# Strassen's seven products for the up-projections of a gated MLP, in written order, with tiles moved

## The chip, the cores and the metric

The kernel runs on one core of a Trainium2 chip. The time is device microseconds of one execution; 2133.42 is the median of three runs of the kernel before (2128.67 to 2134.68). TensorE (PE in the profile) multiplies matrices into PSUM; VectorE (DVE), ScalarE (ACT) and GpSimd (POOL) do the elementwise work, and GpSimd reads no PSUM here. SyncE (SP) issues nearly all transfers. Each engine works through its own queue of instructions in order and waits on semaphores of the others.

## The reference

One layer of an encoder over 1024 positions of width 1024, in float32. The change touches its last part, a gated MLP of hidden width 2816 with a convolution over three positions in the gate:

```python
h = rms_norm(x, norm_ffn_g[l])
gp = dwconv_centered(h @ w_ffn_gate[l], ffn_conv_w[l], ffn_conv_b[l])
x = x + (jax.nn.silu(gp) * (h @ w_ffn_up[l])) @ w_ffn_down[l]
```

Before it come an input projection, latent attention over eight heads, a bidirectional RWKV-7 recurrence, and a gated merge of the two, `x = x + (gates[:, :, 0] * y_a + gates[:, :, 1] * y_b) @ w_merge[l]`.

## The kernel before

Data lie transposed: 128 channels on the partitions, 1024 positions along them. A float32 operand of a product is split into a rounded high part and the rest (`split`, L162: a cast on ScalarE at L163, a subtraction on GpSimd or VectorE at L164), and a product is three matmuls, high times high, high times low and low times high (`mmk`, L245, matmuls at L248, L249 and L251), each 128 x 128 weights against 512 columns. A block of 128 rows and all 1024 positions is therefore six matmuls.

The work runs in four stages. Phase A projects the input and prepares the operands of both branches. Phase B runs the recurrence over chunks, with attention and other dense products in between, in an order that a small planner works out (`LATENCY`, `DENSE`, `PACE`, and the loop over `units`); only PE's order is fixed by hand (`manual_schedule` for PE), the other engines' order is made by the scheduler. The gates of the mixture are written to DRAM by `gate_done` (the stores of the last two tiles of 128 channels go out on GpSimd's queue, the others on SP's). Phase C computes the second branch's part of the mixture (`branch`, eight tiles of four blocks) and the merge: for each of eight tiles of 128 channels, eight blocks with the operands `yh`, `yl`; then VectorE adds the residual (L1485), ScalarE scales it to `h2h` (L1488), VectorE takes the rest `h2l` (L1489), and squares are summed on ScalarE and GpSimd (L1493, L1494).

Phase D is the MLP. `GROUPS` cuts the 22 tiles of 128 hidden channels into four groups. For each tile f, PE forms the gate's product `pg` and the up-projection's `pu`, eight blocks each with the operands `h2h`, `h2l`, in PSUM tiles of 1024 columns (`big4`, four of them in all eight banks). VectorE multiplies `pg` by 1/rms (L1517), ScalarE and VectorE do the convolution (L1522 to L1524), ScalarE the silu, GpSimd multiplies by 1/rms (L1527), VectorE by `pu` (L1528), and the result is split into `sh`, `sl`. After a group the down projection adds its products to the residual `x2`: for each of eight output tiles, as many blocks as the group has tiles, and one addition on VectorE (L1535). In the last group each output tile is stored as it is done (L1537). The sum of squares over channels is a float32 product with ones (`mm32`, L192) after the first gate product. Weights come as 128 x 512 floats, 256 KB, two loads ahead (`wload`, L168, its transfer at L171).

The allocation stacks tiles from the left and from the right of each partition's memory, in steps of 32 bytes. On the left `cst`, `b64r` and `vec` take 391 + 128 + 192 floats, so that what follows (`x2`, `yh`, `yl`, `sh`, `sl`) starts 32 bytes past a multiple of 128; on the right the weights and the places `hh0` to `hl7` of `h2h`, `h2l` start 96 past one.

Of the kernel before, what the change touches and what calls it, by code (L numbers as in the profile page):

```python
# [19 lines left out]
D = 1024  # L20
# [4 lines left out]
C = 64  # L25
# [4 lines left out]
GROUPS = ((0, 6), (6, 12), (12, 17), (17, 22))  # L30
# [18 lines left out]
# How long a step of phase B takes to be ready after it has left TensorE's queue, in ns  # L49
# [39 lines left out]
def block_kernel(ctx: ExitStack, tc: tile.TileContext, a):  # L89
# [15 lines left out]
    # ScalarE functions, grouped by table set in the order of emission  # L105
# [4 lines left out]
    def act(out, in_, func, **kw):  # L110
# [3 lines left out]
        if name != cur["set"]:  # L114
            ld = S.preload_act_table_set(name)
            for g in cur["group"]:
                tc.add_manual_dep(ld.ins, g.ins.name, NOSYNC, reason="table set order")
# [3 lines left out]
        i = S.activation(out, in_, func, **kw)  # L121
        tc.add_manual_dep(i.ins, cur["load"].ins.name, NOSYNC, reason="table set order")
# [7 lines left out]
    nc.sync.dma_start(vec, a["vecs"])  # L130
    ident = cst[:, C_ID:C_ID + 128]
# [121 lines left out]
    # x enters the products as x * g; the evacuation of a product multiplies by 1 / rms(x).  # L253
# [119 lines left out]
    # Products with the projection's tiles: a step per 128 rows.  # L373
# [18 lines left out]
    def parted(x, hi=None, lo=None):  # L392
        """512 columns as the sum of two that a pass each carries."""
# [16 lines left out]
    # The rest of the phase runs as threads between the steps of the projection. A thread yields  # L410
    # what its next part waits for: a key of DELAY, or a tile that has to be there.
# [33 lines left out]
    def key_rope():  # L445
# [25 lines left out]
        # the rows that pad the heads' operands to 128: zeros, and the ones that meet the row of maxima  # L471
# [184 lines left out]
    def parts(idle=False):  # L656
        """The parts that are due of the threads that run; a lane runs so many of its threads at a time."""
# [46 lines left out]
    # ---------------------------------------------------------------- phase B  # L704
# [926 lines left out]
```

## Time and profile before

| | |
|---|---|
| median of three runs | 2133.42 us |
| the profiled execution: its span, first to last instruction | 2126.6 us |
| PE busy | 1958.1 us (92%) |
| phase A, 0 to about 320 us: PE busy | 283.8 us |
| phase B, 320 to 1230 us: PE busy | 786.4 us |
| phase D, 1394.2 us to the end | 732.4 us |
| mean granted PE clock | 0.962 |

The page's second part cuts the span into 40 slices of 53 us and gives the busy share of each engine in tenths. A group of the fifth part names line, engine, operation, output and inputs with shapes, the count, busy time, the mean of one in ns, then idle time before it and what ended that. Matmuls overlap, so their durations (389 ns) are longer than the step from one start to the next; the step is read from the starts in the timeline. Weight loads (PEld) are records of their own and run beside the matmuls.

### The profile page before, as it was taken

Reading aid. Unit: us, or ns where it says so; the run is one execution under the profiler, and the core shown is the slowest. Engines: PE = TensorE matmul, PEld = TensorE weight load, DVE = VectorE, ACT = ScalarE, POOL = GpSimd, SP = SyncE. Lnnn points to the kernel's source line nnn. Section 1 sums busy time; section 2 is a strip of 40 time slices with the busy share of each in tenths; the row PEclk is TensorE's granted clock in tenths of the full one; section 3 lists DMA queues with packets and bytes.
Section 4 is the critical chain, followed back from the end, with each engine's and each line's share of the span. In section 5 each row is a group of like instructions: output and inputs, shape, how many; then the busy total and the mean of one; then the engine's idle time right before and its main releaser. Section 6 shows DMA issues by size and latency. Waiting matters only on the chain.

```text
span 2126.6 us, 31745 instructions
## 1 busy us (share of the span) xinstructions
PE 1958.1 (92%) x12280; PEld 1507.2 (71%) x12280; DVE 997.4 (47%) x1560; ACT 843.1 (40%) x1459; POOL 871.8 (41%) x763
## 2 busy tenths in 40 slices
PE   7799999899898779888779999999999999999999
PEld 5566667677666556556557678888888888888887
DVE  8566766626474768667773235232212321221321
ACT  4676564123233546565547644232212211221221
POOL 7344546133233646564546432433323322332331
PEclk9899999899998989999989999999999999999999
DMA  3047447354344334352433685111111111111113
GB/s 144 34 140 230 145 162 219 104 145 113 98 130 125 78 108 106 104 135 79 100 86 91 205 303 189 50 45 50 43 53 50 50 43 52 50 39 56 50 38 117
DMA packets 212551, 221.09 MB, mean 104 GB/s; under 512 B 114152, under 2 KB 138792, under 8 KB 212400
## 3 DMA queue, kind: packets, MB, share of 16 engines
q1 hardware_dynamic: 212080, 218.01, 33.4%
q8 instruction: 97, 1.59, 0.3%
q0 software_dynamic: 320, 1.05, 0.1%
q14 instruction: 54, 0.44, 0.1%
HBM read 151.20 MB, written 63.60 MB: 101 GB/s over the span
## 4 chain that ended last, share of the span: by engine, by line
PE 51%; DVE 7%; DMA 3%; issue 1%; SPq 1%; POOL 0%; ACT 0%; DVEq 0%; POOLq 0%; ACTq 0%
PE b L251 13%; PE b L248 13%; PE b L249 13%; DMA IN<-dn 2%; DVE Ti L815 2%; DVE tm L811 2%; DVE mx L1151 1%; PE po L1179 1%; PE st L1205 1%; PE po L1181 1%; PE st L1207 1%; PE po L1180 1%; PE st L1206 1%; PE ct L972 1%; PE st L248 1%
## 5 line engine op out<-in xcount | busy, mean ns | idle before, releaser
L164 POOL TENSOR_TENSOR wlo<-wraw,whi 128x512 fp32r<-128x512 f32 x248 | 306.8, 1240 | 792.6 <-ACT whi L163 788.7
L163 ACT CAST whi<-wraw 128x512 fp32r<-128x512 f32 x248 | 145.2, 586 | 652.4 <-PE b L249 462.1
L248 PE MATMUL b<-h2h,whi 128*128 128x512 f32 x704 | 274.3, 390 | 0.0
L249 PE MATMUL b<-h2l,whi 128*128 128x512 f32 x704 | 273.9, 389 | 0.0
L1217 POOL TENSOR_TENSOR pl<-pe,ph 128x512 fp32r<-128x512 f32 x128 | 169.6, 1327 | 131.2 <-ACT ph L1216 128.6
L251 PE MATMUL b<-h2h,wlo 128*128 128x512 f32 x704 | 216.7, 389 | 0.0
L248 PE MATMUL st<-hh,whi 128*128 128x512 f32 x408 | 176.0, 431 | 15.2 <-ACT hh L275 9.0
L249 PE MATMUL st<-hl,whi 128*128 128x512 f32 x408 | 164.7, 404 | 0.5 <-DVE hl L276 0.5
L248 PEld LDWEIGHTS b<-h2h,whi 128*128 128x128 f32 x704 | 132.2, 188 | 27.7 <-issue 0.2
L249 PEld LDWEIGHTS b<-h2l,whi 128*128 128x128 f32 x704 | 132.2, 188 | 27.7 <-issue 0.2
L251 PEld LDWEIGHTS b<-h2h,wlo 128*128 128x128 f32 x704 | 132.2, 188 | 27.5
L251 PE MATMUL st<-hh,wlo 128*128 128x512 f32 x408 | 140.9, 400 | 0.5 <-POOL wlo L164 0.5
L248 PE MATMUL b<-sh,whi 128*128 128x512 f32 x352 | 138.8, 394 | 0.0
L249 PE MATMUL b<-sl,whi 128*128 128x512 f32 x352 | 138.7, 394 | 0.0
L1535 DVE TENSOR_TENSOR x<-b,x 128x1024 f32<-128x1024 f32 x32 | 39.2, 1225 | 197.6 <-PE b L251 197.6
L811 DVE TENSOR_TENSOR tm<-IN,Ti 128x126 f32<-128x126 f32 (+22 forms) x248 | 91.2, 368 | 77.5 <-DMA IN<-dn 71.3
L251 PE MATMUL b<-sh,wlo 128*128 128x512 f32 x352 | 110.4, 394 | 0.0
L248 PEld LDWEIGHTS st<-hh,whi 128*128 128x128 f32 x408 | 79.6, 195 | 43.0 <-issue 9.8
L815 DVE TENSOR_TENSOR Ti<-Ti,tm 128x126 f32<-128x126 f32 (+22 forms) x248 | 104.3, 421 | 6.6
L1517 DVE TENSOR_TENSOR u<-b,rs 128x1024 f32<-128x1024 f32 x22 | 26.9, 1224 | 169.6 <-PE b L251 158.4
L1216 ACT CAST ph<-pe 128x512 fp32r<-128x512 f32 x128 | 79.1, 620 | 64.5 <-PE po L1181 61.3
L980 POOL TENSOR_TENSOR sm<-RR,pcs 64x128 f32<-64x128 f32 x112 | 47.6, 425 | 126.4 <-DVE RR L1002 105.2
(333 smaller groups left out, 4159.1 us busy)
## 6 DMA issues: line engine op xcount, KB each, us to landing
wraw<-w_in SPq DMA_DIRECT2D x64, 256.0 KB
wraw<-w_fg SPq DMA_DIRECT2D x44, 256.0 KB
wraw<-w_fu SPq DMA_DIRECT2D x44, 256.0 KB
ld<-d_x SPq DMA_DIRECT2D x32, 256.0 KB
wraw<-w_fd SPq DMA_DIRECT2D x32, 256.0 KB
d_gate<-gt SPq DMA_DIRECT2D x28, 256.0 KB
xt<-xT SPq DMA_DIRECT2D x8, 512.0 KB
d_s<-sg SPq DMA_DIRECT2D x8, 512.0 KB
```

The costliest lines, as they stand in the source:

```text
L163: S.copy(hi, x)
L164: (eng or G).tensor_tensor(out=lo, in0=x, in1=hi.bitcast(F32), op=sub)
L248: nc.tensor.matmul(o, wh, xh[:, hs], start=first, stop=False)
L249: nc.tensor.matmul(o, wh, xl[:, hs], start=False, stop=False)
L251: nc.tensor.matmul(o, wl, xh[:, hs], start=False, stop=last)
L811: t = V.tensor_tensor(out=tm[:, 0:nt, 0:nj], in0=IN[:, s, s + 1:32][:, :, None].to_broadcast([128, nt, nj]), in1=Ti[:, s, 0:nj][:, None, : ...
L815: V.tensor_tensor(out=Ti[:, s + 1:32, 0:nj], in0=Ti[:, s + 1:32, 0:nj], in1=tm[:, 0:nt, 0:nj], op=add)
L980: state["pool"] = G.tensor_tensor(out=sm[hs], in0=RR[hs, :, h, 0, :], in1=pcv[hs, i // 4, :, i % 4, None].to_broadcast([64, 2, C]), op=mult)
L1216: S.copy(ph, pe)
L1217: G.tensor_tensor(out=pl, in0=pe, in1=ph.bitcast(F32), op=sub)
L1517: V.tensor_tensor(out=u, in0=pg, in1=rs2, op=mult)
L1535: V.tensor_tensor(out=x2[:, j, :], in0=ps, in1=x2[:, j, :], op=add)
```

## The change

Phase D's two up-projections of a tile are read as one product of a 2 x 2 matrix of blocks (up and gate weights, each in two halves of 512 input channels) with a 2 x 2 matrix of blocks of `h` (two halves of channels, two halves of 512 positions). Its eight block products are replaced by seven, in Winograd's form of Strassen's method: `B11`, `B21`, `B22` are blocks of `h`, `U1` to `U4` sums and differences of blocks, made once during the merge; the sums of the weights are made for every tile on GpSimd (`sums_next`, `diffs_next` and the subtraction of `s2`) and split on ScalarE and VectorE (`parts`). A `quarter` is one such product, four blocks of 128 rows against 512 positions, twelve matmuls into one PSUM bank. The results come as sums that build on each other in the banks `ba`, `bb`, `bc`: VectorE reads a partial sum, PE adds the next quarter onto it.

Every engine's order in this block is the written one (`manual_schedule` for all five), the table loads too. The first two tiles run together ahead of the loop, with the last merge tile's evacuation, and the rest of `U4`'s making, among them. From f = 2 each tile's loop also does half of the down products of the pair of tiles before, in units of one output tile, 512 positions and two blocks (six matmuls, `down`, `into`), with the last pair after the loop. `x2` is divided by 1/rms at the start (`over`, on GpSimd) and multiplied by it again before each half tile's store (`finish`), so that 1/rms is not multiplied into the up-projection. The merge evacuates in PSUM and sums the squares on VectorE.

Pads of 32 and 64 bytes move the tiles: the left and the right stack now start 64 bytes past a multiple of 128, and so do the operands of all these products. The room comes from the scratch of GpSimd's descriptors (16384 to 1024 bytes), and the gate stores that went out on GpSimd's queue go out on ScalarE's. Comments are removed throughout. The diff, cut to its core:

```diff
-GROUPS = ((0, 6), (6, 12), (12, 17), (17, 22))
...
             ld = S.preload_act_table_set(name)
+            if "ordered" in cur:
+                cur.update(set=name)
+                return S.activation(out, in_, func, **kw)
...
+    cp.tile([128, 8], F32, name="pad")
...
+    ctx.enter_context(pool("pr", side="right")).tile([128, 8], F32, name="pad")
...
-                (G if j >= 14 else nc.sync).dma_start(d_gate[j][:, hs], gt)
+                (S if j >= 14 else nc.sync).dma_start(d_gate[j][:, hs], gt)
...
+        wk.tile([128, 16], F32, tag="pad", name="pad")
...
+        wk.tile([128, 16], F32, tag="pad2", name="pad")
...
+        eq.tile([128, 8], F32, tag="pad", name="pad")
...
+    B11, U1, B21, B22 = in_hp(0, "b11"), in_hp(2, "t1"), in_hp(4, "b21"), in_hp(6, "b22")
+    U2, U3 = in_pool(bq, "t2", 0), in_pool(bq, "t3", 4)
...
+    def scaled(dst, src, g):
+        S.activation(dst[0], src, AF.Copy, scale=g)
+        V.scalar_tensor_tensor(out=dst[1], in0=src, scalar=g, in1=dst[0].bitcast(F32), op0=mult, op1=sub)
...
+    def sums(j, ps, d):
+        t3, t2 = t5("u3"), t5("u2")
+        V.scalar_tensor_tensor(out=t3, in0=ps[:, HT[1]], scalar=vc("gffn", j), in1=d, op0=mult, op1=sub)
+        V.scalar_tensor_tensor(out=t2, in0=x2[:, j % 4, HT[0]], scalar=vc("gffn", j % 4), in1=t3, op0=mult, op1=add)
+        return t3, t2
...
+    def squares(j, ps):
+        S.copy(x2[:, j, :], ps)
+        if j == 0:
+            S.activation(acc, ps, AF.Square)
+        else:
+            S.activation(ps, ps, AF.Square)
+            V.tensor_tensor(out=acc, in0=ps, in1=acc, op=add)
...
+        V.tensor_tensor(out=ps, in0=ps, in1=x2[:, j, :], op=add)
...
+    ctx.enter_context(tc.manual_schedule(engines={getattr(mybir.EngineType, n) for n in ("PE", "DVE", "Activation", "Pool", "SP")}))
+    cur["ordered"] = True
...
+    def parts(x, eng=V):
+        n = npart[0] % 4
+        npart[0] += 1
+        if n < 2:
+            hi, lo = (wpool["w"].tile([128, 512], R, tag=t, name=t) for t in ("whi", "wlo"))
+        else:
+            hi, lo = (fp.tile([128, 512], R, tag=t, name=t, bufs=2) for t in ("wh", "wl"))
+        split(x, hi, lo, eng)
+        return hi, lo
+    def quarter(b, w, xs, first=False):
+        for k, (xh, xl) in enumerate(xs):
+            ws = slice(k * 128, (k + 1) * 128)
+            for m, (wt, x) in enumerate(((w[0], xh), (w[0], xl), (w[1], xh))):
+                nc.tensor.matmul(b, wt[:, ws], x, start=(first and k == 0 and m == 0), stop=(k == 3 and m == 2), skip_group_check=True)
...
+    w1a = parts(a11)
+    yqs.close()
...
+    V.tensor_tensor(out=ps7, in0=ps7, in1=x2[:, 7, :], op=add)
+    w5a = parts(s1)
+    quarter(ba[0], w1a, B11, True)
+    s2, s3 = f5("s2"), f5("A21")
+    G.tensor_tensor(out=s2, in0=s1, in1=a11, op=sub)
+    G.tensor_tensor(out=s3, in0=a11, in1=a21, op=sub)
+    b11 = load("w_fu", 1, 0, f5("AA"))
+    b22 = load("w_fg", 1, 1, f5("A22"))
+    b21 = load("w_fg", 1, 0, wraw())
+    quarter(bc[0], w5a, U1, True)
+    t3, t2 = sums(7, ps7, d7)
+    scaled(B21[3], ps7[:, HT[0]], vc("gffn", 7))
+    w1b = parts(b11)
+    s1b = gtile("s1b")
+    G.tensor_tensor(out=s1b, in0=b21, in1=b22, op=add)
+    quarter(ba[1], w1b, B11, True)
+    a12 = load("w_fu", 0, 1, wraw())
+    split(t2, *U2[3], V)
+    w5b = parts(s1b)
+    split(t3, *U3[3], V)
+    p1a = t5("p1")
+    S.copy(p1a, ba[0])
+    G.tensor_tensor(out=s1b, in0=s1b, in1=b11, op=sub)
+    G.tensor_tensor(out=b21, in0=b11, in1=b21, op=sub)
+    quarter(bc[1], w5b, U1, True)
+    w2a = parts(a12)
+    scaled(B22[3], ps7[:, HT[1]], vc("gffn", 7))
+    squares(7, ps7)
+    b12 = load("w_fu", 1, 1, f5("AA"))
...
+    def u4(k):
+        t = t5("u3")
+        V.scalar_tensor_tensor(out=t, in0=x2[:, 4 + k, HT[0]], scalar=vc("gffn", 4 + k), in1=U2[k][0].bitcast(F32), op0=mult, op1=sub)
+        V.tensor_tensor(out=t, in0=t, in1=U2[k][1].bitcast(F32), op=sub)
+        split(t, *U4[k], V)
...
+    quarter(ba[0], w2a, B21)
+    for hs, b in zip(HT, db[1:]):
+        nc.tensor.matmul(b, ones, acc[:, hs], start=True, stop=True)
+    w6a = parts(s2)
+    G.tensor_tensor(out=s2, in0=a12, in1=s2, op=sub)
+    p1b = fp.tile([128, T], F32, tag="sl", name="p1b", bufs=3)[:, HT[0]]
+    S.copy(p1b, ba[1])
+    w7a = parts(s3)
+    u4(0)
+    quarter(bb, w6a, U2, True)
+    for hs, b in zip(HT, db[1:]):
+        act(irs[:, hs], b, AF.Ln, scale=1.0 / D, bias=eps)
+    w2b = parts(b12)
+    w4a = parts(a22)
+    act(rs2, irs, AF.Exp, scale=-0.5)
+    act(irs, irs, AF.Exp, scale=0.5)
+    u2a = t5("u2")
+    V.tensor_tensor(out=u2a, in0=bb, in1=p1a, op=add)
+    u4(1)
+    quarter(bb, w7a, U3)
+    w3a = parts(s2)
+    u4(2)
+    u4(3)
+    quarter(ba[1], w2b, B21)
...
+    def u22(u3, p1, c):
+        u = fp.tile([128, T], F32, tag="u", name="u")
+        V.tensor_tensor(out=u[:, HT[1]], in0=c, in1=u3, op=add)
+        V.tensor_tensor(out=u[:, HT[1]], in0=u[:, HT[1]], in1=rs2[:, HT[1]], op=mult)
+        return u
+    def u21(u, p1):
+        V.tensor_tensor(out=bb, in0=bb, in1=p1, op=add)
+        V.tensor_tensor(out=u[:, HT[0]], in0=bb, in1=rs2[:, HT[0]], op=mult)
+    def center(f, u):
+        cv[f] = fp.tile([128, T], F32, tag="cv", name="cv")
+        S.activation(cv[f], u, AF.Identity, scale=vc("cw1", f), bias=vc("cb", f))
+    def taps(f, u, i):
+        o, x, n = ((cv[f][:, 1:], u[:, :-1], "cw0"), (cv[f][:, :-1], u[:, 1:], "cw2"))[i]
+        V.scalar_tensor_tensor(out=o, in0=x, scalar=vc(n, f), in1=o, op0=mult, op1=add)
+    def silu(f):
+        act(cv[f], cv[f], AF.Silu)
+    def left(f, b):
+        sh[f], sl[f] = (fp.tile([128, T], R, tag=t, name=t, bufs=3) for t in ("sh", "sl"))
+        V.tensor_tensor(out=b, in0=b, in1=cv[f][:, HT[0]], op=mult)
+        S.copy(sh[f][:, HT[0]], b)
+    def right(f, b, c, u2, between=None):
+        V.tensor_tensor(out=c, in0=c, in1=u2, op=add)
+        V.tensor_tensor(out=c, in0=c, in1=cv[f][:, HT[1]], op=mult)
+        if between:
+            between()
+        S.copy(sh[f][:, HT[1]], c)
+        for x, hs in zip((b, c), HT):
+            V.tensor_tensor(out=sl[f][:, hs], in0=x, in1=sh[f][:, hs].bitcast(F32), op=sub)
...
+    u3a = t5("u3")
+    V.tensor_tensor(out=u3a, in0=bb, in1=p1a, op=add)
+    u = u22(u3a, p1a, bc[0])
+    w6b = parts(s1b)
+    G.tensor_tensor(out=s1b, in0=b12, in1=s1b, op=sub)
+    quarter(bb, w4a, U4)
+    w7b = parts(b21)
+    u21(u, p1a)
+    center(0, u)
+    over((0,))
+    quarter(bc[0], w3a, B22)
+    taps(0, u, 0)
+    w4b = parts(b22)
+    taps(0, u, 1)
+    silu(0)
+    over((1,))
+    quarter(bb, w6b, U2, True)
+    left(0, ba[0])
+    right(0, ba[0], bc[0], u2a)
+    w3b = parts(s1b)
+    u2 = t5("u2")
+    V.tensor_tensor(out=u2, in0=bb, in1=p1b, op=add)
+    x = load_next(2)
+    over((2,))
+    quarter(bb, w7b, U3)
+    u3 = t5("u3")
+    V.tensor_tensor(out=u3, in0=bb, in1=p1b, op=add)
+    u = u22(u3, p1b, bc[1])
+    s1 = sums_next(*x)
+    W = [parts(x[0])]
+    s2 = diffs_next(x[0], x[1], s1)
+    quarter(bb, w4b, U4)
+    W.append(parts(s2))
+    u21(u, p1b)
+    center(1, u)
+    over((3,))
+    quarter(bc[1], w3b, B22)
+    x12 = load("w_fu", 2, 1, f5("AA"))
+    d1 = load_down(0, 0)
+    taps(1, u, 0)
+    taps(1, u, 1)
+    W.append(parts(x12))
+    silu(1)
+    left(1, ba[1])
+    s3, s22 = x[1], x[2]
...
+    for f in range(2, NF):
+        b, c, last = ba[f % 2], bc[f % 2], f == NF - 1
+        f0, j0 = (f // 2 - 1) * 2, f % 2 * 4
+        quarter(b, W.pop(0), B11, True)
+        right(f - 1, ba[1 - f % 2], bc[1 - f % 2], u2, lambda: W.append(parts(s3)))
+        d2 = load_down(f0, j0 + 2)
+        quarter(bb, W.pop(0), U2, True)
+        p1 = t5("p1")
+        S.copy(p1, b)
+        W.append(parts(d1, G))
+        u2 = t5("u2")
+        V.tensor_tensor(out=u2, in0=bb, in1=p1, op=add)
+        quarter(b, W.pop(0), B21)
+        G.tensor_tensor(out=s2, in0=x12, in1=s2, op=sub)
+        W.append(parts(s1))
+        if f == 2:
+            over((4, 5))
+        if last:
+            d1 = load_down(NF - 2, 0)
+        quarter(bb, W.pop(0), U3)
+        W.append(parts(s22))
+        u3 = t5("u3")
+        V.tensor_tensor(out=u3, in0=bb, in1=p1, op=add)
+        W.append(parts(d2, G))
+        if last:
+            d2 = load_down(NF - 2, 2)
+        else:
+            x = load_next(f + 1)
+        for v in units(W.pop(0), j0):
+            e = dbank()
+            for k in range(2):
+                down(v, f0, k, e)
+            into(v, e)
+        quarter(c, W.pop(0), U1, True)
+        W.append(parts(s2))
+        if not last:
+            s1 = sums_next(*x)
+        u = u22(u3, p1, c)
+        quarter(bb, W.pop(0), U4)
+        W.append(parts(d1, G) if last else parts(x[0]))
+        if last:
+            d1 = load_down(NF - 2, 4)
+        else:
+            s2 = diffs_next(x[0], x[1], s1)
+        if f == 2:
+            over((6, 7))
+        u21(u, p1)
+        if not last:
+            W.append(parts(s2))
+        center(f, u)
+        todo = []
+        for v in units(W.pop(0), j0 + 2):
+            e = dbank()
+            for k in range(2):
+                down(v, f0, k, e)
+            todo.append((v, e))
+            if len(todo) < 3:
+                into(*todo[-1])
+                taps(f, u, len(todo) - 1)
+            else:
+                into(*todo[-1])
+        if last:
+            W.append(parts(d2, G))
+            d2 = load_down(NF - 2, 6)
+        else:
+            x12 = load("w_fu", f + 1, 1, f5("AA"))
+            d1 = load_down(((f + 1) // 2 - 1) * 2, (f + 1) % 2 * 4)
+        quarter(c, W.pop(0), B22)
+        W.append(parts(d1, G) if last else parts(x12))
+        silu(f)
+        left(f, b)
+        s3, s22 = x[1], x[2]
...
+    f0 = NF - 2
+    w = [W.pop(0)]
+    us = units(w[0], 0) + units(W.pop(0), 2)
+    free = db + [bb, ba[0], bc[0], ba[1], bc[1]]
+    for v, e in zip(us[:6], free):
+        down(v, f0, 0, e)
+    right(NF - 1, ba[1], bc[1], u2, lambda: W.append(parts(d2, G)))
+    def finish(v, e):
+        j, hs = v[0:2]
+        into(v, e)
+        V.tensor_tensor(out=x2[:, j, hs], in0=x2[:, j, hs], in1=rs2[:, hs], op=mult)
+        nc.sync.dma_start(a["outT"][j * 128:(j + 1) * 128, hs], x2[:, j, hs])
+    us += units(W.pop(0), 4)
+    for i, v in enumerate(us + units(W.pop(0), 6)):
+        e = free[i % 8]
+        for k in range(i < 6, 2):
+            down(v, f0, k, e)
+        finish(v, e)
...
-    nc = bacc.Bacc("TRN2", target_bir_lowering=False, num_devices=1)
+    nc = bacc.Bacc("TRN2", target_bir_lowering=False, num_devices=1, dynamic_dma_scratch_size=1024)
```

More of the change, by code (lines that the diff above doesn't have):

```diff
@@ new lines, in block_kernel @@
+    ps7, two_ = big4()
+    d7 = scaled_b12(7)
+    merge7 = product(two_, a["w_merge"][7], yx)
+    for _ in range(5):
+        next(merge7)
+    a11 = load("w_fu", 0, 0, wraw())
+    a21, a22 = (load("w_fg", 0, h, rs2[:, HT[h]]) for h in range(2))
+    s1 = gtile("s1")
+    G.tensor_tensor(out=s1, in0=a21, in1=a22, op=add)
+    for _ in merge7:
+        pass
+    w1a = parts(a11)
+    yqs.close()
+    fp = ctx.enter_context(pool("fp"))
+    U4 = in_pool(fp, "t4", 0)
+    bank = [b for _ in range(3) for b in big4()[1]]
@@ new lines, in block_kernel @@
+    irs = place("rstd", "irs", F32)
+    quarter(ba[0], w2a, B21)
[10 more added lines that the diff above has]
+        act(irs[:, hs], b, AF.Ln, scale=1.0 / D, bias=eps)
@@ new lines, in over, with load_next, sums_next, diffs_next @@
+    def over(js):
+        for j in js:
+            G.tensor_tensor(out=x2[:, j, :], in0=x2[:, j, :], in1=irs, op=mult)
+    def load_next(f):
+        x11 = load("w_fu", f, 0, f5("AA"))
+        x21 = load("w_fg", f, 0, f5("A21"))
+        x22 = load("w_fg", f, 1, f5("A22"))
+        return x11, x21, x22
+    def sums_next(x11, x21, x22):
+        s1 = gtile("s1")
+        G.tensor_tensor(out=s1, in0=x21, in1=x22, op=add)
+        return s1
+    def diffs_next(x11, x21, s1):
+        s2 = f5("s2")
+        G.tensor_tensor(out=s2, in0=s1, in1=x11, op=sub)
+        G.tensor_tensor(out=x21, in0=x11, in1=x21, op=sub)
+        return s2
```

123 lines of the change are left out of this document (69 added, 54 removed).

## The prediction

> **What bounds the kernel now.** I read the page first, then the waits from the start of the feed-forward block to the end, then the block's matmuls in order of time.
>
> ```profile
> span 2126.6 us, 31745 instructions
> ...
> PE 1958.1 (92%) x12280; PEld 1507.2 (71%) x12280; DVE 997.4 (47%) x1560; ACT 843.1 (40%) x1459; POOL 871.8 (41%) x763
> ...
> PE   7799999899898779888779999999999999999999
> ...
> PEclk9899999899998989999989999999999999999999
> ```
>
> TensorE (PE) is busy nine tenths or more of every slice from the 23rd on. The waits after 1390 us say who waits for whom (total, times, longest):
>
> ```profile
> DVE x L1535 <- PE b L251: 197.6, 32, 7.2
> DVE u L1517 <- PE b L251: 158.4, 21, 9.7
> DVE sg L1528 <- PE b L251: 121.9, 21, 5.8
> ...
> PEld b L249 <- issue: 0.2, 1, 0.2
> ```
>
> Everything waits for TensorE, and TensorE for nothing over 0.2 us. So this stage's time is a number of matmuls times the step from one start to the next. Counts come from the groups (each of these lines has two siblings of the same count), steps from rows of the timeline (start, duration):
>
> ```profile
> L248 PE MATMUL b<-h2h,whi 128*128 128x512 f32 x704 | 274.3, 390 | 0.0
> ...
> L248 PE MATMUL b<-sh,whi 128*128 128x512 f32 x352 | 138.8, 394 | 0.0
> ...
> L248 PE MATMUL b<-yh,whi 128*128 128x512 f32 x128 | 50.4, 394 | 0.0
> ```
>
> ```profile
> 1380.24 0.39 PE L248 MATMUL b<-yh,whi 128*128 128x512 f32 x1
> ...
> 1392.85 0.39 PE L248 MATMUL b<-yh,whi 128*128 128x512 f32 x1
> ...
> 1394.24 0.39 PE L248 MATMUL b<-h2h,whi 128*128 128x512 f32 x1
> ...
> 2001.28 0.39 PE L248 MATMUL b<-h2h,whi 128*128 128x512 f32 x1
> ...
> 2013.52 0.39 PE L248 MATMUL b<-h2h,whi 128*128 128x512 f32 x1
> ...
> 2112.84 0.40 PE L248 MATMUL b<-sh,whi 128*128 128x512 f32 x1
> ...
> 2119.84 0.40 PE L248 MATMUL b<-sh,whi 128*128 128x512 f32 x1
> ```
>
> Between the two `yh` rows lie 54 matmuls (nine blocks of six): 12.61 / 54 = 0.2335 us. Between 2001.28 and 2013.52 also 54: 0.2267. Between the `sh` rows 30: 0.2333. The block starts at 1394.24, so it takes 2126.6 - 1394.2 = 732.4 us, of which 2112 x 0.2267 + 1056 x 0.2333 = 725.2 is matmuls.
>
> ```profile
> 1420.00:1520.00 100.00, 100.00 (x442) 82.81 (x442) 29.25 (x25) 26.51 (x32) 33.05 (x23) 1.00 0.15 49
> 1530.00:1580.00 50.00, 50.00 (x216) 40.06 (x215) 7.77 (x7) 6.16 (x12) 12.16 (x12) 1.00 0.17 48
> ```
>
> The columns are length, PE, weight loads, DVE, ACT, POOL, granted clock, DMA share, GB/s. At a clock of 1.00 in both stretches, the same 512-column product steps at 0.2267 in one and 0.2333 in the other. What differs is where the operands lie: in this program's allocation `h2h`, `h2l` and the weights start 96 bytes past a multiple of 128, `yh`, `yl`, `sh`, `sl` 32 past one. So the step depends on the place of the operands.
>
> **The change, part by part.**
>
> *Seven products for eight.* A tile's two up-projections are 96 matmuls; seven quarters of 4 x 3 are 84. That removes 22 x 12 = 264, at 0.2267 worth 59.8 us. 1848 + 1056 = 2904 remain.
>
> *Tiles moved.* The pads put both stacks at 64 past a multiple of 128, so every operand of these products moves. No operand in the trace starts there, so I bound the step. The upper ends are 0.2333 and 0.2267. The lower one is the fp32 sum of squares, which passes 512 columns twice in each of four records:
>
> ```profile
> 1405.14 1.88 PE L192 MATMUL b<-acc,ones 128*128 128x512 f32 x4
> ...
> L192 PE MATMUL b<-acc,ones x4: 591/592/592, 1405.1 to 1406.4; 128*128 128x512 f32 x4
> ```
>
> (1.88 - 0.592) / 3 / 2 = 0.2147 per pass. It reads half as fast, from operands at 96 and at 32, and shows no such excess; so the excess of 0.012 to 0.019 belongs to reading at full rate. I estimate that starts on whole 64 bytes remove most of it and take 0.2175, near the fp32 row; the ends stay 0.2147 and 0.2333. The Trainium skill (TensorE: Matmul & The Clock Gate, "Wait — 56ns, not 53.3ns?") measured 215.7 ns for 512 columns back to back; all steps here are above that, and with it the block would be an estimated 2904 x 0.0018 = 5 us shorter.
>
> *The steady tiles, f = 2 to 21.* PE needs 84 + 48 = 132 x 0.2175 = 28.7 us a tile. The other engines' rows:
>
> ```profile
> L897 DVE TENSOR_TENSOR Er<-sc,cst 128x512 f32<-128x512 f32 x32 | 21.6, 686 | 10.3 <-PE sc L896 10.2
> ...
> L1524 DVE SCALAR_TENSOR_TENSOR cv<-u,vec,cv 128x1023 f32<-128x1023 f32 x22 | 29.2, 1326 | 0.8
> L1523 DVE SCALAR_TENSOR_TENSOR cv<-u,vec,cv 128x1023 f32<-128x1023 f32 x22 | 28.2, 1284 | 28.9 <-ACT cv L1522 28.9
> ...
> L163 ACT CAST whi<-wraw 128x512 fp32r<-128x512 f32 x216 | 134.0, 620 | 595.8 <-PE b L249 421.0 <-issue 92.9 <-PE po L249 33.9
> L115 ACT ACT_TABLE_LOAD x29 | 37.2, 1283 | 1.2 <-PEq L1624 0.7
> L1522 ACT ACTIVATE cv<-u,vec 128x1024 f32<-128x1024 f32 x22 | 27.4, 1245 | 22.0 <-DVE u L1517 22.0
> L121 ACT ACTIVATE sg<-cv 128x1024 f32<-128x1024 f32 x22 | 23.3, 1057 | 2.8 <-DVE cv L1524 2.8
> ...
> L164 POOL TENSOR_TENSOR wlo<-wraw,whi 128x512 fp32r<-128x512 f32 x216 | 288.2, 1335 | 767.5 <-ACT whi L163 766.8
> ```
>
> ```profile
> L164 DVE TENSOR_TENSOR sl<-sg,sh x22: 1224/1225/1226, 1421.4 to 2067.8; 128x1024 fp32r<-128x1024 f32 x22
> L164 DVE TENSOR_TENSOR lo<-q,hi x16: 676/928/1644, 112.2 to 343.1; 128x512 fp32r<-128x512 f32 x16
> ```
>
> DVE gets seven weight remainders at 0.93 (the median where POOL is busy), 19 other operations of 512 at 0.69 and two taps at 1.3: 22.2 us. ACT gets twelve of 512 at 0.62 plus 2.3: 9.7. POOL six at 1.34: 8.0. Six loads of 256 KB a tile stand for 5.5 before, at a DMA share of 0.15. All of it fits under 28.7 us. What can stall is the order. Counted from a tile's first quarter, DVE, still at `silu` and `left` of the tile before, ends `right` after about 4.5 us; ACT's copy of P1 is done at 3.7, wanted at 5.2; `u2` at 6.1, wanted at 7.8; `u3` at 11.3, wanted at 18. I take no stall, with 1.5 us a tile as the price if that slack is gone.
>
> *The first two tiles* have no such lead, because each product into bank `bb` adds onto the last, so it waits until DVE has read the sum there; DVE in turn stands behind ACT in written order. In PE's order the waits are: (a) the fourth quarter, for weights whose tiles only come free when the merge ends: 1. (b) tile 0's U3 for `u2a`: behind the squares DVE and ACT do two remainders, one `u4`, a table load, two logarithms and two casts, about 9.0, against 4.5 of PE: 4.5. (c) tile 0's U4 for the other three `u4` and `u3a`: 9.5 against two quarters, 5.2: 4.3. (d) tile 1's U3 for its `u2`, which stands behind all of tile 0's convolution: 0.2 + `u21` 1.37 + center 1.25 + taps 2.61 + `silu` 1.06 + `left` 0.69 + `right` 2.75 and a cast 0.62 + two remainders 1.86 + `u2` 0.69 = 13.1, against 5.2: 7.9. (e) tile 1's U4 for `u3`: 1. (f) tile 2's third quarter, for P1's copy behind tile 1's `right`: 2.2. Together 21 us; it may be 10 if ACT and DVE overlap better, 40 if these gaps also lower the clock.
>
> *End.* Before:
>
> ```profile
> 2121.43 1.22 DVE L1535 TENSOR_TENSOR x<-b,x 128x1024 f32<-128x1024 f32 x1 [5.77 <-PE b L251]
> 2122.68 0.33 SPq L1537 DMA_DIRECT2D outT<-x  x1
> ```
>
> After, each of 16 half outputs costs DVE two operations, 1.37, for 1.3 of PE, and the first six come from half their products: DVE ends 0.7 + 5.6 us after PE, and the last store, half as large, takes about 3.3 of the 3.9 that it took: 9.6.
>
> Sum of the block: 2904 x 0.2175 = 631.6, sum of squares 1.9, first tiles 21, end 9.6: 664.1. It was 732.4, so 68.3 saved.
>
> *Outside it.* The merge's 384 matmuls go from 0.2335 to 0.2175 and the second branch's 192 from 0.2267: 7.9. Its DVE work rises from 2.5 to about 6.5 us an output tile, under 48 x 0.2175 = 10.4 of PE. Before it, 1632 matmuls (the `st` and `po` groups with their siblings) and 768 of attention would gain 0.0092 each, 22 us, if PE were the bound:
>
> ```profile
> 0.00:320.00 320.00, 283.81 (x1073) 203.42 (x1074) 208.83 (x196) 199.74 (x275) 162.26 (x107) 0.96 0.42 142
> 320.00:1230.00 910.00, 786.35 (x7359) 581.37 (x7357) 549.49 (x1159) 417.90 (x890) 423.36 (x443) 0.93 0.43 121
> ...
> L248 PE MATMUL st<-hh,whi 128*128 128x512 f32 x408 | 176.0, 431 | 15.2 <-ACT hh L275 9.0 <-DVE cq L352 6.1 <-ACT whi L163 0.2
> ...
> L1179 PE MATMUL po<-ph,vhh 128*128 128x512 f32 x128 | 65.6, 512 | 2.7 <-ACT pe L121 1.5 <-ACT pc L1184 1.1
> ...
> L248 PE MATMUL po<-hh,whi 128*128 128x512 f32 x136 | 54.6, 401 | 0.0
> ```
>
> PE idles 36 and 124 us there, and the recurrence's steps wait for other engines, so I take half, 11. The four gate stores moved from POOL's queue to ACT's queue stand before ACT's next exponential or cast and wait for DVE's evacuation; at 0.33 us an issue they cost 0 to 1.3 us, and I take nothing because ACT has 490 us free there.
>
> Total 68.3 + 7.9 + 11 = 87.2: a span of 2039.4. The median of the runs is 2133.42, 6.8 above the profiled span; with the same 6.8 the forecast is 2046.
>
> **Rivals.**
>
> *The move does nothing for reading.* Alike offsets of stream and weights give 0.2267, and nothing less. For it: none of these products steps below that for long, and `h2h` and its weights already share their offset. Against it: the fp32 row. Then the block loses 26.7 of the saving, the merge and branch 5.3, the early stages 11: 2046 + 43 = 2089.
>
> *Mixed places.* The seven quarters stream from both sides of memory with weights from both sides; if the distance between them set the step, all go to 0.2333: 2046 + 45.9 + 9.1 + 19 = 2120.
>
> *A stall in every tile*, the slack above being too thin: 20 x 1.5 = 30, 2076; with 3 us, 2106.
>
> *DVE becomes the bound (slower).* It goes from 0.29 busy (1420 to 1520) to 22.2 of 28.7. The `lo` row shows one and the same operation at 0.68 and at 1.64 us where POOL worked beside it; `sl`, with POOL mostly idle, never varies. If all 26 operations of 512 were drawn out to 1.3 us (POOL's own duration), a tile would take 26 x 1.3 + 2.6 = 36.4, plus 20 x 7.7 = 154: 2200. It decides for slower than before from about 33 us a tile, 1.17 us an operation; only ten of the 28 read both inputs from SBUF. The Trainium skill (SBUF — State Buffer, "Who interferes with whom") has the rule that speaks against this change: a DVE instruction with two SBUF inputs contends with a GpSimd instruction that reads SBUF, and the second one blocks. The two rows agree with it.
>
> **How the numbers follow.** Forecast 0.55; nothing from the move 0.28; mixed places 0.05; a stall in every tile 0.08; DVE bound 0.04. The forecast's own ends are 2010 (0.2147, 10 us of stalls, all 22 us early) and 2065 (40 us of stalls). The range 2010 to 2100 adds the first rival with 10 us more stalls and most of the third. About 0.3%, 6.4 us, is what a measurement here can tell from no change: faster 0.95, within it 0.01, slower 0.04.
>
> **What would show it.** Right: 2904 products of 512 columns in the block, stepping near 0.2175 in steady tiles; PE waiting for DVE at three or four places in the first 70 us, the longest near 8 us; none over 1 us in steady tiles; DVE near 0.77 busy; DVE, not PE, last at the end. A step of 0.2267 is the first rival, of 0.2333 the second. PE idle in each tile behind DVE, with remainders over 1.1 us, is the last. I am wrong as a whole if steady tiles take over 31 us or the first two lose over 40.

## The result, and the profile after

The changed kernel takes 2230.86 us (median of six runs, 2222.66 to 2237.08) against 2133.27 for the kernel before on the same chip: a ratio of 1.0472 (95% interval 1.0452 to 1.0491), so 4.7% slower. The forecast was 2046, with a range up to 2100.

The page of the changed kernel, the rows that answer to those shown of before:

```profile
span 2235.3 us, 31847 instructions
...
PE 1945.8 (87%) x12016; PEld 1468.7 (66%) x12016; DVE 1320.8 (59%) x2097; ACT 911.6 (41%) x1587; POOL 815.4 (36%) x718
...
PE   7799999899897788887799899778888989898887
...
PEclk9899999899998889989899999889999999999999
```

PE has 264 products fewer and a longer span: from the 27th slice on it is busy 7 to 9 tenths where it was 9 throughout. DVE at 59% is not full either. The waits from 1395 us on say between which instructions that happens (total, times, longest):

```profile
PEld b L1747 <- DVE x L1759: 79.0, 52, 2.6
PE b L1747 <- DVE x L1759: 57.0, 46, 2.1
...
PEld b L1587 <- DVE sl L1712: 18.0, 10, 1.8
...
PE b L1587 <- DVE sl L1712: 13.8, 10, 1.4
PEld b L1587 <- ACT sh L1703: 11.7, 14, 5.7
PE b L1587 <- DVE u L1680: 11.4, 11, 2.6
...
PE b L1587 <- DVE u L1782: 6.8, 1, 6.8
...
PE b L254 <- ACT whi L168: 5.8, 1, 5.8
PE b L1587 <- ACT sh L1703: 5.3, 1, 5.3
...
PE b L1587 <- DVE u L1667: 4.8, 1, 4.8
```

Before, PE waited for nothing over 0.2 us here. (PEld and PE rows of one place overlap, so they aren't added.) The first two say that down products (L1747) wait for the addition of other down products to the residual (`into`, L1759); the last four are single waits of the last merge tile and of the first two tiles. One steady tile in the timeline of TensorE:

```profile
1772.16 0.50 PE L1587 MATMUL b<-b11h,wh 128*128 128x512 f32 x1
...
1801.21 0.50 PE L1747 MATMUL b<-sh,whi 128*128 128x512 f32 x1 [2.00 <-DVE x L1759]
1801.55 0.40 PE L1748 MATMUL b<-sl,whi 128*128 128x512 f32 x1
...
1802.68 0.63 PE L1749 MATMUL b<-sh,wlo 128*128 128x512 f32 x1
1803.10 0.63 PE L1747 MATMUL b<-sh,whi 128*128 128x512 f32 x1
...
1808.50 0.50 PE L1587 MATMUL b<-b11h,wh 128*128 128x512 f32 x1
...
1812.91 0.50 PE L1587 MATMUL b<-t2h,whi 128*128 128x512 f32 x1 [1.38 <-DVE sl L1712]
...
1823.51 0.50 PE L1747 MATMUL b<-sh,wh 128*128 128x512 f32 x1 [0.78 <-DVE x L1759]
```

and of VectorE:

```profile
1799.27 1.28 DVE L1694 SCALAR_TENSOR_TENSOR cv<-u,vec,cv 128x1023 f32<-128x1023 f32 x1
1800.47 0.68 DVE L1759 TENSOR_TENSOR x<-b,x 128x512 f32<-128x512 f32 x1
...
1811.56 1.29 DVE L1712 TENSOR_TENSOR sl<-b,sh 128x512 fp32r<-128x512 f32 x2 [0.90 <-PE b L1587]
```

The tile lasts 1808.50 - 1772.16 = 36.34 us, for 132 products. At 1801.21 PE starts the moment the addition of the unit before it ends (1800.47 + 0.68), and that addition stood behind a tap of 1.28 us in the written order. Yet a unit (the six matmuls of one output tile and 512 positions) reads nothing of the unit before, and it writes another bank. What joins the two, as the first experiment below shows: `bank = [b for _ in range(3) for b in big4()[1]]` (L1606) cuts PSUM tiles of 1024 columns into halves of one bank each, and waits are set for a whole tile. `ba` are the halves of one tile; `bb` shares one with `bc[0]`, `bc[1]` with `db[0]`, `db[1]` with `db[2]`. Units go to `db[0]`, `db[1]`, `db[2]` in turn. So a unit into `db[2]` waits until the unit before has been read out of `db[1]`; and tile f's U2 into `bb` (row 1812.91) waits for the remainder that `right` takes out of the other tile's `bc[0]`. In the kernel before, both halves of a tile belonged to one product and were read together.

Behind the 2.00 us wait the products step 0.42 instead of 0.23 for 3.4 us (1802.26 to 1805.66). The granted clock, the seventh entry of this row by stretch (length, PE, weight loads, DVE, ACT, POOL, clock), was 0.50 there; it was 1.00 in the 29 us before the wait:

```profile
1802.30:1805.60 3.30, 3.30 (x9) 2.58 (x8) 0.74 (x2) 0.08 (x1) 0.00 (x0) 0.50 0.00 0
```

So a pause can cost a second time, through the clock. From 1518 to 2166 us, some 18 tiles, the starts in the timeline give 60 steps over 0.65 us, together 82.2 us above the usual step, and 140 steps of 0.3 to 0.65, 20.1 us above it. With the rest at 0.228 that is 5.8 us a tile.

Where the time went against the forecast, in us, from starts of products (the end counts from one step behind the last start):

| part of the block | forecast | after |
|---|---|---|
| its start | 1375.3 | 1415.3 |
| first two tiles | 59.4 | 69.1 |
| 20 steady tiles | 574.2 | 717.6 |
| last 96 down products | 20.9 | 28.6 |
| end | 9.6 | 4.7 |

### The profile page after: what moved, and what is told of

Read it like the earlier page. It is cut to its first block, busy times and chain, and to the rows that moved or that the text cites. A ratio compares the mean times of both kernels' runs of the same rounds, so it can differ in the third digit from the quotient of the medians.

```text
span 2235.3 us, 31847 instructions
## 1 busy us (share of the span) xinstructions
PE 1945.8 (87%) x12016; PEld 1468.7 (66%) x12016; DVE 1320.8 (59%) x2097; ACT 911.6 (41%) x1587; POOL 815.4 (36%) x718
## 3 DMA queue, kind: packets, MB, share of 16 engines
q1 hardware_dynamic: 215984, 218.01, 32.7%
## 5 line engine op out<-in xcount | busy, mean ns | idle before, releaser
L169 POOL TENSOR_TENSOR wlo<-wraw,whi 128x512 fp32r<-128x512 f32 x118 | 161.0, 1365 | 564.9 <-ACT whi L168 553.4
L1759 DVE TENSOR_TENSOR x<-b,x 128x512 f32<-128x512 f32 x176 | 121.2, 689 | 108.6 <-PE b L1749 108.6
L168 ACT CAST whi<-wraw 128x512 fp32r<-128x512 f32 x118 | 72.8, 618 | 140.2 <-PE po L255 38.6
L1747 PE MATMUL b<-sh,wh 128*128 128x512 f32 x176 | 72.7, 413 | 29.5 <-DVE x L1759 28.8
L1747 PE MATMUL b<-sh,whi 128*128 128x512 f32 x176 | 72.9, 414 | 28.3 <-DVE x L1759 28.3
L123 ACT ACTIVATE pe<-st 128x512 f32<-128x512 f32 x128 | 76.3, 597 | 41.8 <-PE st L1216 35.3
L257 PEld LDWEIGHTS st<-hh,wlo 128*128 128x128 f32 x408 | 79.3, 195 | 20.4 <-POOL wlo L169 2.3
L1159 DVE TENSOR_REDUCE mx<-st 128x1 f32<-128x512 f32 x112 | 73.3, 683 | 32.2 <-PE st L1158 31.9
L255 PEld LDWEIGHTS st<-hl,whi 128*128 128x128 f32 x408 | 80.2, 196 | 17.1 <-DVE hl L282 1.6
L1748 PE MATMUL b<-sl,whi 128*128 128x512 f32 x176 | 70.1, 398 | 0.0
```

The source lines that it names most:

```text
L169: (eng or G).tensor_tensor(out=lo, in0=x, in1=hi.bitcast(F32), op=sub)
L255: nc.tensor.matmul(o, wh, xl[:, hs], start=False, stop=False)
L257: nc.tensor.matmul(o, wl, xh[:, hs], start=False, stop=last)
L1747: nc.tensor.matmul(b, wh[:, ws], xh[:, hs], start=(k == 0), stop=False)
L1748: nc.tensor.matmul(b, wh[:, ws], xl[:, hs], start=False, stop=False)
L1759: V.tensor_tensor(out=x2[:, j, hs], in0=b, in1=x2[:, j, hs], op=add)
```

## The experiments

The theory from the trace (1) was the shared PSUM tile; the rivals were that VectorE and ScalarE are late in their written order anyway (2), and that the clock is the loss (3). Ratios below are to the kernel before in the same session.

**Eight separate banks** (from the changed kernel). The pools of 1024-column tiles are closed after the seventh merge tile; merge tile 7 is evacuated by halves.

```diff
+    pscs[1].close()
+    pscs[0].close()
+    psd = ctx.enter_context(psum("psd"))
+    def bk(i):
+        return psd.tile([128, 512], F32, tag=f"k{i}", name=f"k{i}")
-    ps7, two_ = big4()
+    two_ = ps7 = [bk(0), bk(1)]
...
-    bank = [b for _ in range(3) for b in big4()[1]]
+    bank = [bk(i) for i in (6, 7, 2, 3, 4, 5)]
...
-    bank += big4()[1]
+    bank += [bk(0), bk(1)]
```

> The changed kernel with the eight PSUM banks of the feed-forward block as eight tiles of 512 columns each, where it had four tiles of 1024 whose halves served different products; same order on every engine. In the changed kernel's trace a steady tile takes 35.7 us for 132 x 0.2267 = 29.9 us of products, and the starts that TensorE lost stand behind VectorE's or ScalarE's reading of the other half of the same tile. Theory 1 (each PSUM tile is one object to the waits, so a write to one half waits for the reader of the other): steady tiles of 30 to 31 us, the gap of 5.66 us in front of tile 2's first bank gone, whole time 2231 - 20 x 5.2 - 5 = about 2120, between 2100 and 2140. Theory 2 (VectorE and ScalarE are late in their written order, whatever the bank): steady tiles stay at 35 to 36 us and the time within 10 us of 2231. Theory 3 (the clock is cut, and the waits are small beside it): the waits go but the stretches at half speed stay, 33 to 34 us a tile, about 2190.

Measured: 2100.39, ratio 0.9865 (0.9836 to 0.9895). The row by stretch of the changed kernel and then of this one:

```profile
1518.00:2166.00 648.00, 574.36 (x2394) 448.68 (x2394) 368.69 (x508) 171.54 (x256) 136.79 (x108) 0.99 0.14 44
```

```profile
1497.00:2030.00 533.00, 533.00 (x2354) 441.33 (x2353) 351.44 (x499) 168.67 (x250) 136.91 (x108) 1.00 0.16 54
```

Nearly the work that the changed kernel does in 648 us, on every engine, in 533, and PE without a gap. Two tile starts of its timeline:

```profile
1526.32 0.39 PE L1588 MATMUL k<-b11h,whi 128*128 128x512 f32 x1
...
1556.24 0.39 PE L1588 MATMUL k<-b11h,whi 128*128 128x512 f32 x1
```

29.92 us, which is 132 x 0.2267, and so for each of the last 19 tiles; the gap in front of tile 2's first product is gone too. Theories 2 and 3 are out for these tiles: the written order has room enough, and the half-speed stretches went with the waits. Of the 126.1 us that the block gained (820.0 to 693.9), 115.6 lie in the 20 tiles.

**The down products' pair joined again.**

```diff
+    def pair():
+        t = psd.tile([128, T], F32, tag="k01", name="k01")
+        return [t[:, hs] for hs in HT]
-    two_ = ps7 = [bk(0), bk(1)]
+    two_ = ps7 = pair()
...
-    bank += [bk(0), bk(1)]
+    bank += pair()
```

> The kernel with eight separate banks, but the two banks that only the down products use joined again into one tile of 1024 columns, as in the changed kernel; the other six stay apart. It asks which pair cost the 114 us. In the changed kernel's waits after 1390 us the rows behind VectorE's additions to the residual hold 79.0 + 57.0 us, those behind the other readers about 55. If the loss goes by these rows: some 70% of the 5.8 us a tile, 4 us, so tiles of 33 to 35 us and 2100 + 20 x 4 = 2180, between 2160 and 2190. If the banks of the up-projections carry it: tiles of 30 to 31 us, below 2125.

Measured: 2180.09, ratio 1.0244 (1.0225 to 1.0263); steady tiles of 32.7 to 35.4 us. This kernel differs from the one with eight banks only in that two banks are one allocated tile, and that alone costs 80 us of the 130. In its steady tiles (1520 to 2030 us) PE's waits are of one kind; from 1395 us on they come to:

```profile
PEld k L1764 <- DVE x L1776: 77.8, 49, 3.1
PE k L1764 <- DVE x L1776: 56.8, 43, 2.6
```

The other 50 us go with the three other pairs together; no run joins those one at a time.

**Only the tiles moved** (from the kernel before).

```diff
+    cp.tile([128, 8], F32, name="pad")
...
+    ctx.enter_context(pool("pr", side="right")).tile([128, 8], F32, name="pad")
...
+        wk.tile([128, 16], F32, tag="pad", name="pad")
...
+        wk.tile([128, 16], F32, tag="pad2", name="pad")
...
+        eq.tile([128, 8], F32, tag="pad", name="pad")
```

> The kernel before with the five pads alone: every operand of the three-product matmuls at 64 past a multiple of 128, nothing else changed. By the forecast's step (0.2175 us) the feed-forward block gains 2112 x 0.0092 + 1056 x 0.0158 = 36 us, merge and branch 7.9, early stages up to 22: about 2133 - 55 = 2078, at least 2089 without the early stages. By the rival (only whether stream and weights lie alike counts): products with yh and sh go from 0.2333 to 0.2267, those with h2h stay at 0.2267, so the block gains 1056 x 0.0066 = 7.0 and the merge 384 x 0.0068 = 2.6: 2133 - 9.6 = 2124. If places don't matter at all: 2133, within 3.

Measured: 2113.35, ratio 0.9930 (0.9906 to 0.9954). The second group of down products and the next tiles' first product:

```profile
1519.14 0.39 PE L250 MATMUL b<-sh,whi 128*128 128x512 f32 x1
...
1584.42 0.39 PE L250 MATMUL b<-h2h,whi 128*128 128x512 f32 x1
```

288 products in 65.28 us, 0.2267 each where it was 0.2333; `yh` likewise, and `h2h` stays at 0.2267. No group of these products steps at the forecast's 0.2175. The block gains 7.1 us, the merge 2.5; the other 5 of the 14.6 us by which the span is shorter lie in the two branches' products (3.2; they begin with the group `st<-o`) and before them (1.7). Of the gain those 5 us are not shown to be the pads': where the branches start differs by 6.4 us among this run, the kernel before and the runs with the gate stores and the crossed places.

**Places crossed** (from the kernel before): streams that lay like the weights now don't, and the other way round.

```diff
+    cp.tile([128, 16], F32, name="pad")
...
+    ctx.enter_context(pool("pr", side="right")).tile([128, 16], F32, name="pad")
     hp = ctx.enter_context(pool("hp", side="right"))
```

> The kernel before with two pads of 64 bytes that cross the places: the streams of the up-projections from 96 to 32 past a multiple of 128, the streams of merge and down products from 32 to 96, all weights at 96 as before. If a stream and weights that lie alike step at 0.2267 and others at 0.2333: up-projections 0.2333 (+2112 x 0.0066 = 13.9 us), down products 0.2267 (-7.0), merge 0.2267 (-2.6), second branch 0.2333 (+1.3), and 0 to 11 us more before it: 2134 to 2146. If the side of memory sets the step, or the distance doesn't matter: no group changes and 2129.

Measured: 2134.28, ratio 1.0036 (1.0021 to 1.0051). In its timeline, at the two ends of a group of down products and of six tiles' up-projections:

```profile
1526.81 0.40 PE L250 MATMUL b<-sh,whi 128*128 128x512 f32 x1
...
1592.11 0.39 PE L250 MATMUL b<-h2h,whi 128*128 128x512 f32 x1
...
1726.51 0.39 PE L250 MATMUL b<-sh,whi 128*128 128x512 f32 x1
```

288 products at 0.2267, then 576 in 134.40 us, 0.2333: the two steps changed hands. Not the side of memory decides, but the starts of stream and weights, taken past a multiple of 128 bytes: both at 96 give 0.2267, a stream at 32 with weights at 96 gives 0.2333.

**The changed kernel without its pads.** Its edit takes out the five lines of the pads shown above.

> The changed kernel without its five pads, so that streams and weights lie partly at 96 and partly at 32 past a multiple of 128. If only alikeness of stream and weights counts: products with both sides alike step at 0.2267 and the others at 0.2333, half of them each. Of 132 products in a tile that is 66 x 0.0066 = 0.44 us a tile, 10 us over the block if TensorE's own speed set the tile, near 0 if the waits on the other half of a bank pair set it; the second branch and merge 2.6 us more. Together 2231 + 0 to 13. By the forecast's step the pads would be worth 36 us and more, so 2267 or above. If the pads cost the early stages 12 us: 2219 and a branch that starts near 1256.

Measured: 2241.35, ratio 1.0528 (1.0496 to 1.0559), some 10 us above the changed kernel; its block is 7.9 us longer. In its down products, streams at 32 with weights at 32 have a median of 0.2273 over undisturbed stretches of six steps, with weights at 96 0.2333: 32 alike is about as good as 64 or 96 alike, and whole 64 bytes aren't what counts. This run alone also has streams at 96 with weights at 32 (the quarters of `B11`, `B21`, `B22` and `U1` with weights in `wh`, `wl`). They settle near 0.229, so that places that differ cost some 0.0066 in the one direction and about a third of it in the other, where the expectation had one price for both.

**The gate stores** (from the kernel before).

```diff
-                (G if j >= 14 else nc.sync).dma_start(d_gate[j][:, hs], gt)
+                (S if j >= 14 else nc.sync).dma_start(d_gate[j][:, hs], gt)
...
-    nc = bacc.Bacc("TRN2", target_bir_lowering=False, num_devices=1)
+    nc = bacc.Bacc("TRN2", target_bir_lowering=False, num_devices=1, dynamic_dma_scratch_size=1024)
```

> The kernel before with only the gate stores of the last two tiles on ScalarE's queue and the smaller descriptor scratch. In the changed kernel the second branch's stage starts at 1268.1 us against 1256.2 before. If the stores' new place is the cause: that stage starts 10 to 12 us later and the time is 2143 to 2145. If it is the pads or the order the scheduler chooses with them: 2133, within 4 (the forecast took nothing for the stores).

Measured: 2130.83, ratio 1.0007 (0.9985 to 1.0029). They cost nothing that can be measured, as forecast. Nor does the change itself delay the branches. Their first product (`st<-o`) came at 1208.4 in the changed kernel's profile and at 1194.0 before, but between 1193.5 and 1201.0 in the five other kernels of these experiments that are written like the changed one up to there.

**The last merge tile's weights ahead** (from the eight banks). There and in the changed kernel, PE stood 5.8 us at that tile's start; this is the row of the kernel with eight banks:

```profile
1387.70 0.79 PE L254 MATMUL k<-yh,whi 128*128 128x512 f32 x1 [5.84 <-ACT whi L168]
```

The written order begins at this tile, and its casts stood behind the evacuation of the tile before.

```diff
             pass
+        if j == 6:
+            first.append(wrows(a["w_merge"][7], 0, 8))
         V.tensor_tensor(out=ps, in0=ps, in1=x2[:, j, :], op=add)
```

> The kernel with eight separate banks, and the first weights of the last merge tile loaded and cast ahead of the evacuation of the tile before, in place of behind it. There TensorE stood 6.2 us and then ran at half its step. If ScalarE's written order is the cause: the gap goes, the block starts 8 to 12 us earlier, near 1390, and the time is 2088 to 2093. If the load or the weights' buffer is the cause: the gap stays, 2100.

Measured: 2093.35, ratio 0.9846 (0.9824 to 0.9868). The gap falls to 0.4 us and the merge takes 88.2 us instead of 94.9, so ScalarE's order was the cause. The 6.7 us are less than the 8 to 12 expected, and the two ratios alone, whose intervals overlap, would not show a gain.

**The first two tiles in another order**, two attempts. The first:

```diff
-    w2b = parts(b12)
-    w4a = parts(a22)
+    u2a = t5("u2")
+    V.tensor_tensor(out=u2a, in0=bb, in1=p1a, op=add)
+    w2b = parts(b12, G)
+    w4a = parts(a22, G)
...
-    w3a = parts(s2)
+    w3a = parts(s2, G)
...
     quarter(bb, w6b, U2, True)
-    left(0, ba[0])
-    right(0, ba[0], bc[0], u2a)
+    V.tensor_tensor(out=u2, in0=bb, in1=p1b, op=add)
...
     u = u22(u3, p1b, bc[1])
+    left(0, ba[0])
+    right(0, ba[0], bc[0], u2a)
```

> The kernel of the run with the last merge tile's weights ahead, and the order of the first two tiles changed: tile 0's second sum directly behind its quarter, three remainders of that stretch on GpSimd, and tile 1's two sums ahead of tile 0's gate and its splits. The gaps of 3.6 and 9.7 us in front of the third quarters should fall to 1 to 2 us each, and with the half-speed stretches behind them the first two tiles should take 50 us where they took 62: 2076 to 2084. If VectorE's whole work there is the bound, the gaps only move and it stays at 2088 to 2093.

Measured: 2094.28, ratio 0.9847 (0.9824 to 0.9869): no gain. The two steps of 3.6 and 9.7 us fell to 1.3 and 2.9, the first two tiles took 56.3 us instead of 62.5, but tile 2 took 39.7 instead of 33.5. A new step of 9.1 stood in front of tile 0's product with U4. PE waited there for `u3a`, which stands behind the making of U4 on VectorE, and that waited for ScalarE:

```profile
1421.12 1.06 ACT L123 ACTIVATE rs<-irs 128x1024 f32<-128x1024 f32 x1 [2.66 <-POOL wlo L169]
```

The exponential writes the tile that still holds the weights `a22`, waits for GpSimd's remainder of them, and U4's casts are queued behind it. The second attempt mends that:

```diff
-    u4(0)
+    ts = [t5("u3"), u2]
+    u4(0, ts[0])
+    u4(1, ts[1])
+    u4l(0, ts[0])
     quarter(bb, w6a, U2, True)
...
+    w3a = parts(s2, G)
     for hs, b in zip(HT, db[1:]):
         act(irs[:, hs], b, AF.Ln, scale=1.0 / D, bias=eps)
...
+    W.append(parts(x12))
     center(1, u)
...
+    quarter(ba[0], W.pop(0), B11, True)
+    p1 = t5("p1")
+    S.copy(p1, ba[0])
     taps(1, u, 0)
```

> The kernel with the last merge tile's weights ahead, and the first two tiles ordered anew a second time. In the run before, ScalarE's exponential for 1/rms had to wait until GpSimd had read the weights that lie in the same tile, and the casts for U4 stood behind it. Now U4's four parts are made two at a time with their casts ahead of the logarithms and exponentials, tile 1's sums stand ahead of tile 0's gate, and ScalarE's copy of tile 2's first product ahead of tile 1's silu. If order alone makes these gaps: first two tiles 45 to 50 us where they took 62.5, tile 2 30 to 32 where it took 33.5, together 2093 - 14 = about 2079 (2074 to 2086). If VectorE's total work up to the first steady tile is the bound: the gaps move again and it stays at 2090 to 2095.

Measured: 2091.22 (median of six runs), ratio 0.9829 (0.9803 to 0.9856). This has the lowest median here, 1.7% below the kernel before, but the gain over the two kernels before it is too small to tell from no change. By its trace the first two tiles took 52.3 us instead of 62.5 and tile 2 37.5 instead of 33.5: of 10.2 us gained, 4.0 moved on. The 2079 of the expectation was missed, and the time is that of its other case, VectorE's total work. The trace bears that out in part: VectorE is busy 43.9 of the 52.3 us, and while GpSimd divides the residual, an operation of 0.69 us takes up to 2.8.

## Why the prediction was wrong

*The step that failed* is "I take no stall" for the steady tiles. It set the times when `right`, P1's copy, `u2` and `u3` are done against the times when TensorE wants them, each for its own bank. It asked nothing of the banks of the down products, and not who else lives in the same PSUM tile. The slack that it reckoned was there: with eight separate banks none of the last 19 tiles stalls. But two products that share a PSUM tile are tied to each other's readers. A stall came with every third unit, at 0.8 us (the row at 1823.51) even where VectorE answers at once, and the steady tiles lost 5.8 us each where the forecast had none. The third rival, a stall in every tile, named the right symptom with another cause and at most 3 us. The line that cuts the tiles into banks was there to read in the changed kernel; the trace of before could not show its cost, since there no two products shared a tile. The Trainium skill (PSUM — Partial Sum Buffer, "PSUM bank collisions raise a hardware error") asks to guard PSUM by bank, which is what the faster kernel does; the changed one guarded by pairs of banks, which is safe but ties what needn't be tied. The row with 533.00 of 533.00 us agrees that PE can write one bank while VectorE reads another.

*Tiles moved.* The step of 0.2175 was wrong; it is 0.2267, as the first rival said, and the difference is worth 26.7 us over the block. The fp32 row that the forecast leaned on gave no bound: no group of these products comes near it. The first half of the argument, that the place of the operands sets the step, was right, and the crossing showed what counts: whether the places are alike, rather than whole 64 bytes.

*Seven products for eight* was right: 2904 products, at one step without a stall in the kernel with eight banks.

*The first two tiles* were right in kind: PE waited at most of the places that were named. 21 us of waits were forecast; with eight banks the loss is 62.45 - 168 x 0.2267 - 1.9 = 22.5, and 3.6 more in tile 2. That the sums agree is in part luck: some 17 of the 22.5 us are waits, and the rest are products at about half the clock behind them, which the 21 left out. In the changed kernel the waits (b) and (d) lost 5.0 and 7.0 where 4.5 and 7.9 were forecast (their idle times, 4.8 and 6.8, are the rows with `u L1667` and `u L1782` above); 5.4 us more stood in front of tile 2, behind ScalarE's cast out of the other half of `ba` (the row of 5.3). *The end* was 7.7 us with eight banks where the forecast had 9.6.

*Outside the block* the forecast was 40 us too early. It had 18.9 saved. Instead the merge was 5.4 us longer, with the last merge tile's casts, which the forecast had left out (the written order starts at that tile, and what the scheduler had put ahead before now stands in line). The branches were 1.3 longer. The 11 us of early gain didn't come, and the profiled execution reached the branches 14.4 us later, which the five other profiles of the same early code don't repeat; why this one was late stays open.

*DVE becomes the bound*, the slower rival, was not the cause: it was busy 368.69 of 648 us, and with eight banks the weight remainders on it took 0.71 us in the mean where the forecast had 0.93. The sum of the forecast with 0.2267 in it gives 690.8 us for the block; with eight banks it took 693.9. So the account of the block was sound apart from the step and the tiles that two products shared.

## What to carry to other kernels

Before counting slack, list for each buffer who else lives in the same allocated object, and count the waits of all of them as one: where PE's written order has nothing to spare, such a tie can be a stall. Make a PSUM tile as large as what is read out together. Where a written order takes over from a scheduler, look at what is queued at the border. And a gap that is filled in a chain of several engines often moves to the next link, so count the whole chain before pricing the gain.

## What the runs showed of the hardware

A 512-column product of this kind steps 0.2267 us when stream and weights start alike past a multiple of 128 bytes (both 32, both 64 or both 96). It steps 0.2333 with a stream at 32 and weights at 96, and about 0.229 the other way round, which one run alone has. Other differences were not tried, and the runs don't show why the place counts.

A pause of about 2 us can halve the speed for the 3.4 us behind it (1802.26 to 1805.66 above). In the changed kernel, none of the 36 pauses of 1.0 to 2.0 us up to 2200 us (a pause is what a step takes above 0.2267) was followed by more than one product at half speed; of 13 pauses of 2.0 to 2.6 us five were followed by seven or eight. So a wait costs from its own length to nearly twice that. The Trainium skill (TensorE: Matmul & The Clock Gate, "Part 1: The HAM clock gate (the "warmup" mystery)") gives free-running windows of about 3.4 us and a throttled state after an idle one; the length of the slow stretch agrees, while pauses shorter than a window were enough here.

In the last kernel, VectorE beside GpSimd:

```profile
1434.43 2.82 DVE L169 TENSOR_TENSOR wlo<-A,whi 128x512 fp32r<-128x512 f32 x1
```

```profile
1431.02 8.45 POOL L1739 TENSOR_TENSOR x<-x,irs 128x1024 f32<-128x1024 f32 x3
```

The remainder, which reads both inputs from SBUF, took four times its 0.68. The second of GpSimd's three operations ended at 1436.70 and the remainder at 1437.25, as if it had waited for that one to finish. That is what the forecast's slower rival feared. It occurs in the first tiles, where GpSimd has long operations; none of the 125 remainders on VectorE in this kernel's steady tiles (1490 to 2020 us) took over 1 us.
